# The first gate chunk of a fused attention step, multiplied in two halves of 256 tokens, with its weights loaded ahead of two token tiles

## The chip, the cores and the metric

The kernel runs on one core of a Trainium2 chip. The metric is device time in microseconds, from launch to end. The kernel before takes 711.55 us, the median of three runs (711.53 to 712.34).

## The reference

One step of a hybrid diffusion backbone with one trunk layer. There are 1152 tokens of width 1024: 128 context tokens (tile 0) and 1024 latent tokens (tiles 1 to 8, 128 tokens each). Everything is float32.

```python
shift, scale, gate = modulation(cond, w_mod[l], b_mod[l])      # silu(cond) @ w_mod + b_mod
h = rmsnorm(x, norm_gain[l]) * (1.0 + scale) + shift
q_a, k_a, v_a, g_a, q_b, k_b, v_b, g_b = project(h, w_in[l], ...)
o_a = global_attn_latent(q_a, k_a, v_a, ...)
o_b = window_attn_latent(q_b, k_b, v_b, ..., sink_b[l])
x = x + gate * concat([o_a * silu(g_a), o_b * silu(g_b)]) @ w_out[l]
```

The change touches only the beginning: rmsnorm and modulation of the first token tiles, and the product that gives `g_a`, the gates of head group A (512 columns of `w_in`).

## The kernel before, in words

**Arithmetic.** A matrix product is made of three products of rounded parts: high part of the activations by high part of the weights, high by low, low by high. A high part is a cast (`whi`, `h_at(0, ...)`), the low part is what the cast left out (`wlo`, `h_at(1, ...)`).

**A token tile's way in.** `load_x(t)` (L366) fetches a tile of 128 tokens by 1024 from the SP queue into one of four `xn` buffers. `squares(t)` (L370) has ACT square and sum it (L373) and POOL turn the sum into 1/rms (L375, L377). `scaled(t)` (L379) has DVE multiply the tile by it (L380). `turned_tile(t)` (L382) has PE transpose it in eight 128x128 blocks, four to each of two PSUM banks `px` (L390). `keep(t, c, copy)` (L392) copies bank c into `xT`; ACT takes the first bank and DVE the second, mostly.

**Modulation of a row chunk.** Width 1024 is cut into eight chunks of 128 rows, called k or j. For chunk j, `modulate_rows(j)` (L342) multiplies the condition by the slice `wm[j]` (1 MB, loaded by `load_wm`, in two halves for chunk 0) in 16 small matmuls (L346) and has it copied to `mrows` (L349). `modulate(j)` (L351) transposes that (L355), and DVE makes of it a scale `a_mod` and a shift `b_col` (L357, L359, L361). `modulated(j, t0, n, cond)` (L396) applies them to n tiles from tile t0: ACT writes the high part of h (L403), DVE the same in full (`hf`, L404), POOL the difference (L405).

**Gate products.** `W_GA.load()` (L214) fetches 256 KB of weights for a chunk, `W_GA.split()` (L230) casts them on ACT (L234) and subtracts on DVE or POOL (L236). `gate_products` (L253) makes the three products for one group of 128 gate columns `ch`: high parts at L263 and L264, the low part of h at L259. There are four groups, each with a PSUM bank for tiles 1 to 4 (512 tokens, `big`, through `first_gates`) and a half bank for tiles 5 and 6 (256 tokens, `small`, through `next_gates`); each sums over the eight chunks.

**Order.** Everything is written out by hand; the engines run their instructions in the order of the program, each waiting on semaphores. Ahead of the loop over j (L467), tiles 1 to 4 go through squares, scaling and transposes, chunk 0 is modulated for all four tiles, and its weights are split. Iteration j of the loop makes the gate products of chunk j - 1 for the 512 tokens, has chunk j modulated between them, brings in another tile (tile 5 in j = 1, tile 6 in j = 2, then 7, 8 and 0), and makes the products for tiles 5 and 6 of chunk j - 2. `warm(n)` (L420) issues n matmuls on an identity matrix whose result nobody reads.

**SP queue.** All loads stand in one queue: x tiles 1 to 4, `wm[0]` in two halves, the first gate weights, x tile 5, `wm[1]` and so on (L407 to L418). A load into a buffer waits there until its last reader is through, and every load waits for the one eight places ahead of it to land.

Of the kernel before, what the change touches and what calls it, by code (L numbers as in the profile page):

```python
# [58 lines left out]
WARM = (8, 4)  # L59
# [49 lines left out]
def hybrid_step(ctx, tc, x_prompt, x_sample, cache_k_a, cache_v_a, cache_k_b, cache_v_b,  # L109
# [33 lines left out]
    def bank(tag, name):  # L143
        return ps.tile([P, 512], F32, tag=tag, name=name, bufs=BANKS[tag])
# [108 lines left out]
    def gate_products(out, w, ch, ts, k, first=True, last=True, part=None):  # L253
        cs = slice(P * ch, P * ch + P)
        if part != 1:
            gate_high(out, w, cs, ts, k, first)
        if part != 0:
            i, to = third(ts)
            nc.tensor.matmul(out, w.hi[k][:, cs], h_at(1, i, k, to), start=False, stop=(k == KT - 1 and last))  # L259
# [52 lines left out]
    with tc.tile_pool(name="st", bufs=2, side="right") as st:  # L312
# [11 lines left out]
        def load_wm(j):  # L324
            w = st.tile([P, KT, 2, P], F32, tag="wm", name=f"wm{j}", bufs=3)
            for ks in (slice(0, 4), slice(4, 8)) if j == 0 else (slice(0, 8),):
                nc.sync.dma_start(w[:, ks], w_mod_ss[j][:, ks])
            wm.append(w)
# [13 lines left out]
        def modulate_rows(j):  # L342
            pm = pmod[j] = bank_tr(f"pm{j}")
            for k in range(KT):
                a = 32 * (k % 4)
                nc.tensor.matmul(pm[a : a + 32, 0:256], sil32[:, k, :], wm[j][:, k].rearrange("p s n -> p (s n)"),  # L346
                                 start=(k < 4), stop=(k >= 4), tile_position=(0, a))
            mrows[j] = st.tile([P, 256], F32, tag="mrows", name=f"mrows{j}")
            (nc.scalar.copy if j > 1 else nc.vector.tensor_copy)(mrows[j], pm[:, 0:256])  # L349

        def modulate(j):  # L351
            pm = pmod.pop(j)[:, 256:512]
            for s in range(2):
                cs = slice(P * s, P * s + P)
                nc.tensor.transpose(pm[:, cs], mrows[j][:, cs], ident)  # L355
            m4 = st.tile([P, 2, 2], F32, tag="m4", name=f"m4_{j}")
            nc.vector.tensor_reduce(m4, pm.rearrange("p (s g c) -> p s c g", s=2, c=32)[:, :, 0:2, :], axis=AX.X,  # L357
                                    op=ALU.add)
            nc.vector.tensor_scalar(a_mod[:, j, :], m4[:, 0], bsc1[:, j : j + 1], colt[:, 16 + j : 17 + j],  # L359
                                    op0=ALU.add, op1=ALU.mult)  # L360
            nc.vector.tensor_scalar(b_col[:, j, :], m4[:, 1], colt[:, 24 + j : 25 + j], None, op0=ALU.add)  # L361
# [4 lines left out]
        def load_x(t):  # L366
            xn[t] = st.tile([P, D], F32, tag="xn", name=f"xn{t}", bufs=4)
            nc.sync.dma_start(xn[t], x_tile[t])
# [10 lines left out]
        def scaled(t):  # L379
            nc.vector.tensor_scalar(xn[t], xn[t], rx.pop(t), None, op0=ALU.mult)  # L380

        def turned_tile(t, tags, between=None):  # L382

            for c in range(2):
                if c and between:
                    between()
                px[t, c] = bank(tags[c], f"px{t}_{c}")
                for i in range(4):
                    k = 4 * c + i
                    nc.tensor.transpose(px[t, c][:, P * i : P * i + P], xn[t][:, P * k : P * k + P], ident)  # L390

        def keep(t, c, copy):  # L392
            at = slice(P * place(t), P * place(t) + P)
            copy(xT[:, 4 * c : 4 * c + 4, at], px.pop((t, c)).rearrange("p (k n) -> p k n", n=P))

        def modulated(j, t0, n, cond):  # L396

            w = P * n
            dst = slice(P * place(t0), P * place(t0) + w)
            i, to = third(dst)  # L400
            a, b = (x[:, j, cond : cond + 1] for x in (a_mod, b_col))
            hf = st.tile([P, 512], F32, tag="hf", name=f"hf{j}_{t0}", bufs=3)
            nc.scalar.activation(h_at(0, i, j, to), xT[:, j, dst], AF.Identity, scale=a, bias=b)  # L403
            nc.vector.tensor_scalar(hf[:, :w], xT[:, j, dst], a, b, op0=ALU.mult, op1=ALU.add)  # L404
            nc.gpsimd.tensor_tensor(h_at(1, i, j, to), hf[:, :w], h_at(0, i, j, to), op=ALU.subtract)  # L405

        for t in (1, 2, 3, 4):  # L407
            load_x(t)
        load_wm(0)
        W_GA.load()  # L410
        load_x(5)
        load_wm(1)
        load_x(6)
        W_GA.load()
        load_wm(2)
        W_GA.load()
        load_x(7)
# [2 lines left out]
        def warm(n):  # L420

            idle = bank("D", "idle")
            for _ in range(n):
                nc.tensor.matmul(idle, ident_b, ident_b.unsqueeze(1).to_broadcast([P, 4, P]), start=True, stop=True)

        second = [x for k in range(KT) for x in ((k, 7, 2, 0), (k, 0, 1, 1))]

        def first_gates(ch, k, part=None):
            gate_products(big[ch], W_GA, ch, slice(0, 512), k, part=part)

        def next_gates(ch, k):
            o = 256 * (ch % 2)
# [5 lines left out]

        copies = nc.scalar.copy, nc.vector.tensor_copy

        for t in (1, 2, 3, 4):
            squares(t)
        warm(WARM[0])
        for t, tags in ((1, "AB"), (2, "AB"), (3, "CC")):
            scaled(t)
            turned_tile(t, tags)
            if t > 1:
                for c in range(2):
                    keep(t - 1, c, copies[c])
        scaled(4)  # L450
        modulate_rows(0)
        keep(3, 0, copies[0])
        W_GA.split(nc.gpsimd)
        turned_tile(4, "AB", lambda: modulate(0))
        keep(4, 0, copies[0])
        modulated(0, 1, 4, 0)
        keep(3, 1, copies[1])
        keep(4, 1, copies[1])
        load_wm(3)
        load_x(0)  # L460
        squares(5)
        warm(WARM[1])
        big = [bank("AABB"[ch], f"pg0_{ch}_f") for ch in range(4)]
        sg_tile.append(lambda n: st.tile([P, 512], F32, tag="sg", name=n))
        rest = {3: 7, 4: 8, 5: 0}

        for j in range(1, KT + 2):  # L467
            big_on, small_on = j <= KT, 2 <= j
            if 1 < j < KT:
                W_GA.split()  # L470
            if j == KT + 1:
                put_gates(big[0], 0, 0, slice(0, 512))
            if big_on:
                first_gates(0, j - 1, 0)
                first_gates(1, j - 1, 0)
            if j == 2:
                turned_tile(6, "CC")
                for c in range(2):
                    keep(6, c, copies[c])
                small = [bank("C", f"pg0_{ch}_s") for ch in (0, 2)]  # L480
                for k in range(2):
                    modulated(k, 5, 2, 0)
            if j < KT:
                modulate_rows(j)
                if j + 3 < KT:
                    load_wm(j + 3)
            if j == 1:
                scaled(5)
                squares(6)
            if j in rest:  # L490
                scaled(rest[j])
            if j + 1 in rest:
                squares(rest[j + 1])
            if big_on:
                first_gates(0, j - 1, 1)
                first_gates(1, j - 1, 1)
                first_gates(2, j - 1)
            if j < KT:
                modulate(j)
                if j == 1:  # L500
                    W_GA.split()
                modulated(j, 1, 4, 0)
                if j == 1:
                    scaled(6)
            if big_on:
                first_gates(3, j - 1)
            if j == 1:
                turned_tile(5, "DE")
                for c in range(2):
                    keep(5, c, copies[c])  # L510
            if j in rest:
                turned_tile(rest[j], "DE")
                for c in range(2):
                    keep(rest[j], c, copies[c])
            if 1 < j < KT:
                modulated(j, 5, 2, 0)
            for ch in range(4):
                if small_on:
                    next_gates(ch, j - 2)
                if j > SECOND_FROM or (j == SECOND_FROM and ch % 2):  # L520
                    more()
            if KT - 2 <= j < KT:
                raw = st.tile([P, KT, 2, P], F32, tag="wm", name=f"raw_qa{j}", bufs=3).rearrange(
                    "p (k a) s n -> p k (a s n)", a=2)
                k0 = 4 * (j - KT + 2)
                c0, n = W_QA.cols[0]
                nc.sync.dma_start(
                    raw, w_in[P * k0 : P * k0 + 512, c0 : c0 + n].rearrange("(k p) n -> p k n", p=P))
                W_QA.raw += [raw[:, k] for k in range(4)]
# [816 lines left out]
```

## Time and profile before

| what | value |
|---|---|
| median of three runs | 711.55 us |
| profiled execution, first to last instruction | 709.6 us |
| PE busy | 691.6 us, 97% |
| DVE, ACT, POOL busy | 469.3, 409.9, 334.2 us |
| first transpose of tile 1 | at 8.18 us |
| first gate product | at 16.98 us |
| first gate product of chunk 1 (iteration j = 2) | at 22.34 us |
| `wm[0]` issued from 3.52 us, its second half landed | 8.7 us after its issue |

In the profile PE is the matrix engine, PEld its weight loads, DVE the vector engine, ACT the scalar engine, POOL the GpSimd engine, SP the engine that issues most loads. A row of the timeline has the start in us, the duration in us, the engine, the source line, the operation, the tile written and those read, their shapes, how many instructions are merged (x16: the duration runs from the first's start to the last's end), and in brackets how long the engine sat idle before and who released it. Buffer numbers are left out of names. A matmul's duration overlaps the next one's, so its cost in a row of matmuls is the distance between two starts.

### The profile page before, as it was taken

Reading aid. Unit: us, or ns where it says so; the run is one execution under the profiler, and the core shown is the slowest. Engines: PE = TensorE matmul, PEld = TensorE weight load, DVE = VectorE, ACT = ScalarE, POOL = GpSimd, SP = SyncE. Lnnn points to the kernel's source line nnn. Section 1 sums busy time; section 2 is a strip of 40 time slices with the busy share of each in tenths; the row PEclk is TensorE's granted clock in tenths of the full one; section 3 lists DMA queues with packets and bytes.
Section 4 is the critical chain, followed back from the end, with each engine's and each line's share of the span. In section 5 each row is a group of like instructions: output and inputs, shape, how many; then the busy total and the mean of one; then the engine's idle time right before and its main releaser. Section 6 shows DMA issues by size and latency. Waiting matters only on the chain. (4 is left out here: it accounts for less than half of the span.)

```text
span 709.6 us, 10604 instructions
## 1 busy us (share of the span) xinstructions
PE 691.6 (97%) x3508; PEld 558.5 (79%) x3508; DVE 469.3 (66%) x1019; ACT 409.9 (58%) x829; POOL 334.2 (47%) x356
## 2 busy tenths in 40 slices
PE   7999999999999999989999999999999999999987
PEld 4778988878787889966788888888888888787865
DVE  4667257967848945647867578666775776675662
ACT  5646412412403431188777887787778777877760
POOL 3547023233213421256756655665576557555660
PEclk9999999999999999999999999999999999999999
DMA  8962283358353116332222121212221221222323
GB/s 316 415 211 102 78 302 74 90 154 263 84 139 104 37 39 215 123 108 57 78 68 85 50 82 53 71 57 75 68 82 38 79 71 50 78 72 70 104 67 121
DMA packets 53560, 78.58 MB, mean 111 GB/s; under 512 B 7096, under 2 KB 25720, under 8 KB 52608
## 3 DMA queue, kind: packets, MB, share of 16 engines
q1 hardware_dynamic: 45328, 65.96, 28.1%
q10 hardware_dynamic: 8176, 11.94, 6.3%
q8 instruction: 28, 0.46, 0.3%
q14 instruction: 28, 0.23, 0.1%
HBM read 58.69 MB, written 19.18 MB: 110 GB/s over the span
## 5 line engine op out<-in xcount | busy, mean ns | idle before, releaser
L1131 POOL TENSOR_TENSOR pl<-pe,ph 128x512 fp32r<-128x512 f32 x130 | 167.7, 1292 | 145.0 <-DVE nm L942 67.5
L882 DVE TENSOR_REDUCE mx<-pmx 128x1 f32<-128x384 f32 x192 | 101.4, 552 | 56.3 <-PE pmx L881 54.8
L1123 ACT ACTIVATE pe<-st 128x512 f32<-128x512 f32 x146 | 86.8, 594 | 28.2 <-PE st L1121 27.4
L1127 ACT CAST ph<-pe 128x512 fp32r<-128x512 f32 x146 | 90.6, 621 | 4.8
L1141 PE MATMUL pv<-ph,v_hi 128*128 128x512 f32 x208 | 82.8, 398 | 2.2 <-DVE spare L1165 2.2
L1144 PE MATMUL pv<-pl,v_hi 128*128 128x512 f32 x208 | 82.4, 396 | 0.0
L1212 PE MATMUL po<-wo,ogh 128*128 128x512 f32 x216 | 72.6, 395 | 0.2 <-DVE yt L1219 0.2
L174 POOL TENSOR_TENSOR rs_q<-ms_q,mhalf 128x8 f32<-128x8 f32 x18 | 34.1, 1896 | 80.9 <-DVE ms_q L172 80.9
L942 DVE CUSTOM_DVE_ANT_0 sn<-sn,mask,nsink 128x512 f32<-128x512 f32 (+1 forms) x64 | 46.4, 724 | 38.0 <-PE sn L939 37.6
L881 PE MATMUL pmx<-kha,qt 128*128 128x384 f32 x192 | 61.2, 363 | 0.4 <-ACT pen L928 0.2
L1120 PE MATMUL st<-qt,kha 128*128 128x512 f32 x144 | 58.2, 404 | 1.9 <-ACT pe L1123 1.1
L1121 PE MATMUL st<-qb,kla 68*128 68x512 f32 x144 | 57.5, 399 | 1.1 <-DVE qb L901 1.1
L1143 PE MATMUL pv<-ph,v_lo 128*64 128x512 f32 x146 | 57.6, 395 | 0.0
L1144 PEld LDWEIGHTS pv<-pl,v_hi 128*128 128x128 f32 x208 | 39.2, 189 | 16.4
L928 ACT ACTIVATE pen<-sn,nm 128x512 f32<-128x512 f32 (+2 forms) x72 | 45.0, 626 | 6.5 <-DVE nm L942 3.1
L1116 ACT CAST ph<-st 128x512 fp32r<-128x512 f32 x62 | 36.4, 587 | 19.9 <-PE st L1115 18.7
L1141 PEld LDWEIGHTS pv<-ph,v_hi 128*128 128x128 f32 x208 | 39.3, 189 | 10.6 <-ACT ogh L1177 2.4
L646 ACT CAST qo0q<-ptq 128x512 fp32r<-128x512 f32 x18 | 10.6, 586 | 60.7 <-PE ptq L643 55.8
L1212 PEld LDWEIGHTS po<-wo,ogh 128*128 128x128 f32 x216 | 40.0, 188 | 6.8 <-DVE yt L1219 0.6
L1117 DVE TENSOR_TENSOR pl<-st,ph 128x512 fp32r<-128x512 f32 x62 | 42.5, 686 | 2.7 <-ACT ph L1116 2.1
L1212 PE MATMUL po<-wo,ogl 128*128 128x512 f32 x108 | 42.6, 394 | 0.0
L881 PEld LDWEIGHTS pmx<-kha,qt 128*128 128x128 f32 x192 | 35.6, 191 | 6.4 <-DVE mx L882 1.3
(213 smaller groups left out, 1699.2 us busy)
## 6 DMA issues: line engine op xcount, KB each, us to landing
qt<-qd SPq DMA_DIRECT2D x36, 256.0 KB, 3.0
wm<-in_w_mod_ss_dram SPq DMA_DIRECT2D x7, 1024.0 KB, 10.0
qd<-qo0q ACTq DMA_DIRECT2D x36, 128.0 KB, 2.4
qd<-qo1q ACTq DMA_DIRECT2D x36, 128.0 KB, 2.4
sgl<-gd SPq DMA_DIRECT2D x36, 128.0 KB, 2.2
out_dram<-yt SPq DMA_DIRECT2D x17, 256.0 KB, 2.0
xn<-in_x_sample_dram SPq DMA_DIRECT2D x8, 512.0 KB, 7.2
wg<-in_w_mod_g_dram SPq DMA_DIRECT2D x4, 1024.0 KB, 8.3
```

The costliest lines, as they stand in the source:

```text
L881: nc.tensor.matmul(pm[:, 0:384], lhs, kha[:, g, 3 * b : 3 * b + 3, :], start=True, stop=True)
L882: nc.vector.tensor_reduce(mx[:, h, b : b + 1], pm[:, 0:384], axis=AX.X, op=ALU.max)
L942: nc.vector.tensor_tensor_reduce(s, s, mask[:, m0 : m0 + n], -1.0, nsink[:, 4 * g + h : 4 * g + h + 1], op0=ALU.add, op1=ALU.min, accum_ou ...
L1120: nc.tensor.matmul(s, kh, qtile[i], start=True, stop=False)
L1121: nc.tensor.matmul(s, kl, qbtile[i], start=False, stop=True)
L1123: nc.scalar.activation(pe, s, AF.Exp)
L1127: nc.scalar.copy(ph, pe)
L1131: nc.gpsimd.tensor_tensor(pl, pe, ph, op=ALU.subtract)
L1141: nc.tensor.matmul(pv, two, ph, start=(b == 0), stop=False)
L1143: nc.tensor.matmul(pv[0:64, :], vl, ph, start=False, stop=False)
L1144: nc.tensor.matmul(pv, two, pl, start=False, stop=last)
L1212: nc.tensor.matmul(po[n], a, wo_parts[KT * n + k][lo], start=(k == KS[0] and p == 0), stop=(k == KS[-1] and p == 2))
```

## The change

Loads: x tiles 3 and 4 move behind `wm[0]` and the first gate weights; x tile 5 moves behind `wm[1]` and the second gate weights.

Preparation: only tiles 1 and 2 are squared, scaled and transposed ahead of chunk 0's modulation, and each tile is copied to `xT` right behind its transposes. Chunk 0 is then modulated for tiles 1 and 2 alone, and the products of its high parts with the first 256 tokens are issued. Tiles 3 and 4 are squared behind that modulation, transposed around the products of the low part, and modulated as a second half. The other 256 tokens of chunk 0 are multiplied in the loop's first iteration, where all 512 were before. Chunks 1 to 7 are multiplied by 512 tokens as before. The number of gate products of chunk 0 goes from 12 with 512 tokens to 24 with 256.

```diff
-        for t in (1, 2, 3, 4):
+        for t in (1, 2):
             load_x(t)
         load_wm(0)
         W_GA.load()
+        for t in (3, 4):
+            load_x(t)
+        load_wm(1)
+        W_GA.load()
         load_x(5)
-        load_wm(1)
         load_x(6)
-        W_GA.load()
         load_wm(2)
         W_GA.load()
         load_x(7)
@@
-        def first_gates(ch, k, part=None):
-            gate_products(big[ch], W_GA, ch, slice(0, 512), k, part=part)
+        def first_gates(ch, k, part=None, half=None):
+            ts = slice(0, 512)
+            if k == 0:
+                ts = slice(256 * (half or 0), 512 if half is None else 256 * half + 256)
+            gate_products(big[ch][:, ts], W_GA, ch, ts, k, half != 1, part=part)
@@
-        for t in (1, 2, 3, 4):
+        for t in (1, 2):
             squares(t)
         warm(WARM[0])
-        for t, tags in ((1, "AB"), (2, "AB"), (3, "CC")):
+        for t, tags in ((1, "AB"), (2, "CC")):
             scaled(t)
             turned_tile(t, tags)
-            if t > 1:
-                for c in range(2):
-                    keep(t - 1, c, copies[c])
+            for c in range(2):
+                keep(t, c, copies[c])
+        big = [bank("AABB"[ch], f"pg0_{ch}_f") for ch in range(4)]
+        modulate_rows(0)
+        W_GA.split(nc.gpsimd)
+        modulate(0)
+        modulated(0, 1, 2, 0)
+        squares(3)
+        squares(4)
+        warm(WARM[1])
+        for ch in range(4):
+            first_gates(ch, 0, 0, 0)
+        scaled(3)
+        turned_tile(3, "CC")
+        for c in range(2):
+            keep(3, c, copies[c])
+        for ch in range(4):
+            first_gates(ch, 0, 1, 0)
         scaled(4)
-        modulate_rows(0)
-        keep(3, 0, copies[0])
-        W_GA.split(nc.gpsimd)
-        turned_tile(4, "AB", lambda: modulate(0))
-        keep(4, 0, copies[0])
-        modulated(0, 1, 4, 0)
-        keep(3, 1, copies[1])
-        keep(4, 1, copies[1])
+        turned_tile(4, "DE")
+        for c in range(2):
+            keep(4, c, copies[c])
+        modulated(0, 3, 2, 0)
         load_wm(3)
         load_x(0)
         squares(5)
-        warm(WARM[1])
-        big = [bank("AABB"[ch], f"pg0_{ch}_f") for ch in range(4)]
@@
-                first_gates(0, j - 1, 0)
-                first_gates(1, j - 1, 0)
+                first_gates(0, j - 1, 0, 1)
+                first_gates(1, j - 1, 0, 1)
```

The remaining calls of `first_gates` in the loop get the same last argument, 1.

The order of ACT ahead of the loop is the first place that matters. In the kernel before, `xn_177`, `xn_179`, `xn_181` and `xn_183` are x tiles 1 to 4, `px_0_*` is the first transposed half of a tile, `whiga` the cast weights, `h_0_0` the high part of h for chunk 0:

```order
L373 ACTIVATE sq_206,ss_207<-xn_177 128x1024
L373 ACTIVATE sq_213,ss_214<-xn_179 128x1024
L373 ACTIVATE sq_220,ss_221<-xn_181 128x1024
L373 ACTIVATE sq_227,ss_228<-xn_183 128x1024
L394 COPY xT<-px_0_244 128x4x128
L394 COPY xT<-px_0_255 128x4x128
L394 COPY xT<-px_0_268 128x4x128
L234 CAST whiga_293<-rawga_188 128x512
L394 COPY xT<-px_0_299 128x4x128
L403 ACTIVATE h_0_0_115<-xT,b_col,a_mod 128x512
L373 ACTIVATE sq_326,ss_327<-xn_190 128x1024
```

In the changed kernel x tiles 3 and 4 are `xn_186` and `xn_188`:

```order
L373 ACTIVATE sq_206,ss_207<-xn_177 128x1024
L373 ACTIVATE sq_213,ss_214<-xn_179 128x1024
L394 COPY xT<-px_0_230 128x4x128
L394 COPY xT<-px_0_243 128x4x128
L234 CAST whiga_270<-rawga_184 128x512
L403 ACTIVATE h_0_0_115<-xT,b_col,a_mod 128x256
L373 ACTIVATE sq_286,ss_287<-xn_186 128x1024
L373 ACTIVATE sq_293,ss_294<-xn_188 128x1024
L394 COPY xT<-px_0_314 128x4x128
L394 COPY xT<-px_0_331 128x4x128
L403 ACTIVATE h_0_0_115<-xT,b_col,a_mod 128x256
```

The squares of tiles 3 and 4 have moved from ahead of the first copy to behind the first modulated h, and h comes in two pieces.

DVE in the same place is the second. Before, with `xn` as above, `rsx` the 1/rms of a tile, and `px_1_*` the second transposed half of a tile:

```order
L380 TENSOR_SCALAR xn_177<-xn_177,rsx_211 128x1024
L380 TENSOR_SCALAR xn_179<-xn_179,rsx_218 128x1024
L394 COPY xT<-px_1_249 128x4x128
L380 TENSOR_SCALAR xn_181<-xn_181,rsx_225 128x1024
L394 COPY xT<-px_1_260 128x4x128
L380 TENSOR_SCALAR xn_183<-xn_183,rsx_232 128x1024
L349 COPY mrows_290<-pm_281 128x256
L357 TENSOR_REDUCE m_0_306<-pm_281 128x4
L359 TENSOR_SCALAR a_mod<-m_0_306,bsc_170,colt 128x2
L361 TENSOR_SCALAR b_col<-m_0_306,colt 128x2
L404 TENSOR_SCALAR hf_1_316<-xT,a_mod,b_col 128x512
```

And in the changed kernel:

```order
L380 TENSOR_SCALAR xn_177<-xn_177,rsx_211 128x1024
L394 COPY xT<-px_1_235 128x4x128
L380 TENSOR_SCALAR xn_179<-xn_179,rsx_218 128x1024
L394 COPY xT<-px_1_248 128x4x128
L349 COPY mrows_268<-pm_259 128x256
L357 TENSOR_REDUCE m_0_278<-pm_259 128x4
L359 TENSOR_SCALAR a_mod<-m_0_278,bsc_170,colt 128x2
L361 TENSOR_SCALAR b_col<-m_0_278,colt 128x2
L404 TENSOR_SCALAR hf_1_282<-xT,a_mod,b_col 128x256
L380 TENSOR_SCALAR xn_186<-xn_186,rsx_291 128x1024
L394 COPY xT<-px_1_319 128x4x128
L380 TENSOR_SCALAR xn_188<-xn_188,rsx_298 128x1024
```

The copy of tile 1's second half now stands between the scalings of tiles 1 and 2, and the scalings of tiles 3 and 4 stand behind the first modulation, with the copy of tile 3 between them.

More of the change, by code (lines that the diff above doesn't have):

```diff
@@ L494, in hybrid_step @@
             if big_on:
-                first_gates(0, j - 1, 1)
-                first_gates(1, j - 1, 1)
-                first_gates(2, j - 1)
+                first_gates(0, j - 1, 1, 1)
+                first_gates(1, j - 1, 1, 1)
+                first_gates(2, j - 1, None, 1)
             if j < KT:
@@ L505, in hybrid_step @@
             if big_on:
-                first_gates(3, j - 1)
+                first_gates(3, j - 1, None, 1)
             if j == 1:
```

## The prediction

> **What bounds the kernel now.** I read first how busy each engine is in the stages around the change, then the timelines of PE, ACT, DVE and POOL ahead of the loop, then the loads. The stages:
>
> ```profile
> 0.00:16.98 16.98, 11.89 (x63) 7.25 (x63) 7.17 (x17) 9.82 (x17) 5.27 (x15) 1.00 0.85 312
> 16.98:22.34 5.36, 5.36 (x38) 3.62 (x39) 3.47 (x9) 3.52 (x7) 2.79 (x5) 1.00 1.03 420
> 22.34:61.00 38.66, 38.59 (x288) 29.35 (x288) 29.41 (x55) 23.19 (x46) 22.41 (x27) 1.00 0.68 256
> 61.00:200.00 139.00, 138.89 (x689) 115.27 (x690) 95.42 (x184) 41.51 (x77) 39.58 (x31) 1.00 0.47 143
> 200.00:400.00 200.00, 194.44 (x977) 160.64 (x976) 132.32 (x326) 104.11 (x224) 88.00 (x88) 1.00 0.31 94
> 400.00:709.60 309.60, 302.42 (x1457) 242.37 (x1455) 201.46 (x432) 227.73 (x464) 176.16 (x194) 1.00 0.23 73
> ```
>
> After stretch and length the columns are busy PE, PEld, DVE, ACT, POOL, granted clock, DMA share, GB/s. From 16.98 us, where the first gate product starts, PE does not pause until 61 us. So the start is a question of one instant: when does PE enter iteration j = 2 (22.34 us before), with the same work left? From there on the programs are alike. PE before that:
>
> ```profile
> 3.36 3.60 PE L424 MATMUL idle<-ident_b 128*128 128x512 bf16 x8 [3.36 <-DVE ident_b L316]
> 8.18 3.68 PE L390 MATMUL px<-ident,xn 128*128 128x128 f32 x16 [1.22 <-DVE xn L380]
> 13.29 1.07 PE L346 MATMUL pm<-wm,sil 128*32 128x256 f32 x16
> 14.91 0.44 PE L355 MATMUL pm<-ident,mrows 128*128 128x128 f32 x2
> 15.19 0.60 PE L390 MATMUL px<-ident,xn 128*128 128x128 f32 x4
> 16.98 0.50 PE L263 MATMUL pg_f<-h,whiga 128*128 128x512 f32 x1 [0.33 <-ACT h L403]
> 17.32 0.40 PE L264 MATMUL pg_f<-h,wloga 128*128 128x512 f32 x1
> 17.56 0.40 PE L263 MATMUL pg_f<-h,whiga 128*128 128x512 f32 x1
> 18.12 1.07 PE L346 MATMUL pm<-wm,sil 128*32 128x256 f32 x16
> 21.30 1.03 PE L390 MATMUL px<-ident,xn 128*128 128x128 f32 x8
> 22.34 0.50 PE L263 MATMUL pg_f<-h,whiga 128*128 128x512 f32 x1
> ```
>
> Two things: the first gate product waits for ACT's h, and tiles 1 and 2 went through PE back to back, 16 transposes in 3.68 us, when eight take 1.03 us later. PE starts at half speed, though the granted clock reads 1.00 throughout.
>
> [...]
>
> **The chain that the change makes.** What a tile needs, taken from tile 3 (first five rows) and from copies and chunk 0's modulation:
>
> ```profile
> 9.13 1.06 ACT L373 ACTIVATE sq<-xn 128x1024 bf16<-128x1024 f32 x1 [1.36 <-DMA xn<-in_x_sample_dram]
> 10.09 0.19 ACT L373 ACTIVATION_READ_ACCUMULATOR sq<-xn 128x1 f32 x1
> 10.37 0.19 POOL L375 TENSOR_SCALAR msx<-ss 128x1 f32<-128x1 f32 x1 [1.54 <-ACT sq L373]
> 10.64 0.55 POOL L377 TENSOR_TENSOR rsx<-msx,mhalf 128x1 f32<-128x1 f32 x1
> 11.22 0.76 DVE L380 TENSOR_SCALAR xn<-xn,rsx 128x1024 f32<-128x1024 f32 x1 [0.34 <-POOL rsx L377]
> ...
> 8.86 0.76 DVE L380 TENSOR_SCALAR xn<-xn,rsx 128x1024 f32<-128x1024 f32 x1 [0.73 <-POOL rsx L377]
> 10.19 0.69 DVE L394 COPY xT<-px 128x512 f32<-128x512 f32 x1 [0.58 <-PE px L390]
> 12.96 0.59 ACT L394 COPY xT<-px 128x512 f32<-128x512 f32 x1 [0.32 <-PE px L390]
> 16.11 0.81 ACT L403 ACTIVATE h<-xT,b_col,a_mod 128x512 fp32r<-128x512 f32 x1 [0.54 <-DVE b_col L361]
> 24.63 1.09 ACT L403 ACTIVATE h<-xT,b_col,a_mod 128x256 fp32r<-128x256 f32 x2
> ```
>
> *Tile 2.* DVE now copies tile 1 ahead of scaling tile 2. The copy cannot start before 10.19, when tile 1's transposes end; it ends at 10.88, the scaling at 11.64 (9.62 before). PE, which went straight on, idles, and transposes tile 2 from 11.65 at the slow rate (8.18 to 10.15 was eight): 13.6.
>
> *Modulation.* Its 16 small matmuls follow. At full speed they take 1.07 us; no row shows them slow, so the bounds are 0.8 us (1.07, overlapping the transposes' end by a quarter microsecond) and 1.8 (1.97 / 1.03 = 1.9 times, same overlap). I take 1.8, PE having just paused: 15.4. From their end (13.29 + 1.07 = 14.36) to h was 1.75 us before; the slow pair at L355 adds some 0.2: h starts at 17.35 and, half as wide, takes 1.09 / 2 = 0.55: 17.9. The first gate products therefore start no earlier than the 16.98 of before.
>
> *Tile 3.* ACT squares tile 3 only behind that h, where before it did so at 9.13. Squares to read-out are 1.15 us (9.13 to 10.28), POOL 0.91 (to 11.19), DVE 0.79 (to 11.98): 17.9 + 2.85 = 20.75. PE meanwhile has its four idle matmuls and eight half-width products, and then waits. POOL's low part of h lies in front of tile 3's mean but ends within the squares:
>
> ```profile
> 25.91 1.48 POOL L405 TENSOR_TENSOR h<-hf,h 128x256 fp32r<-128x256 f32 x2 [1.61 <-DVE hf L404]
> ```
>
> Two of that width take 1.48 us, so one takes 0.74, against 1.15 for the squares.
>
> *Tile 4.* Tile 3's transposes, 1.03 at full speed: 21.8. DVE copies (0.7), then scales tile 4 (0.76): 23.3. The first four transposes (0.60) end at 23.9, ACT copies (0.59) and makes the second half of h (0.55): with hand-offs 25.1. DVE's copy of tile 4 and the four low-part products lie beside this.
>
> *Iteration j = 1.* Products of 256 tokens cost half (the first two rows; the others are ACT's, in j = 1 of before):
>
> ```profile
> 27.64 0.28 PE L264 MATMUL pg_s<-h,wloga 128*128 128x256 f32 x1
> 27.75 0.28 PE L259 MATMUL pg_s<-h,whiga 128*128 128x256 f32 x1
> 20.10 0.60 ACT L234 CAST whiga<-rawga 128x512 fp32r<-128x512 f32 x1
> 21.47 0.82 ACT L403 ACTIVATE h<-xT,b_col,a_mod 128x512 fp32r<-128x512 f32 x1 [0.77 <-DVE b_col L361]
> ```
>
> Start to start 0.11 to 0.12, against 0.24 (17.32 to 17.56) for 512 tokens: twice as many at half the price, nothing on PE's total. Four products bring the second modulation to 25.6, its matmuls to 26.65. Before, 3.15 us lay between their end (19.19) and 22.34, with five wide products ahead of the transposes of its rows; those now save 0.6: 26.65 + 2.55 = 29.2. ACT has tile 5's and 6's squares and a weight cast in between, 2 x 1.15 + 0.6 behind 25.1 = 28.0, before h is due to start, at 28.3 (as much ahead of 29.2 as 21.47 of 22.34). **Sum: 29.2 - 22.34 = 6.9 us late.**
>
> **Loads**, which the change also moves:
>
> ```profile
> L327 SPq DMA_DIRECT2D wm<-in_w_mod_ss_dram x2: 471/537/603, 3.5 to 4.2; - x2
> DMA to landing us min/median/max: 8.7/8.7/8.7
> DMA to landing us min/median/max: 6.4/6.8/7.2
> ...
> 13.89 2.25 SPq L368 DMA_DIRECT2D xn<-in_x_sample_dram x2
> 17.66 0.33 SPq L327 DMA_DIRECT2D wm<-in_w_mod_ss_dram x1
> 29.97 0.42 PE L346 MATMUL pm<-wm,sil 128*32 128x256 f32 x4
> wm<-in_w_mod_ss_dram SPq DMA_DIRECT2D x7, 1024.0 KB, 10.0
> ```
>
> The first pair of rows is `wm[0]`: its second half landed at 4.2 + 8.7 = 12.9. The next row is x tiles 3 and 4 (issued 2.6 and 3.05, landed by 10.3). Without these 1 MB in front, at 312 to 420 GB/s, `wm[0]` lands 2.5 to 3.4 us earlier, about 10. That gains nothing, since tile 2's transposes end at 13.6. Tiles 3 and 4 land 3 to 4 us later, by some 14, which ACT's other work up to 17.9 hides; were that cover gone, each microsecond would cost one. Loads of tiles 7 and 8 (13.89 on, 2.25) wait for buffers of tiles 3 and 4, now until 21.8 and 24; the fourth `wm` (17.66) is queued behind them, to about 25. With the usual 10.0 to land it is there at 35; its matmuls (29.97) are wanted 6.9 later, at 36.9. Cover 1.9 us.
>
> **Forecast.** The profiled execution has 709.6 us of span, the median is 711.55, so 1.95 lie outside. Span 709.6 + 6.9 = 716.5; time 711.55 + 6.9 = **718.4 us**.
>
> **Rivals.**
>
> *PE stays slow longer.* If the pauses (half a microsecond at 15.5, the wait for tile 3) keep PE slow until it runs without pause from about 24, tile 3 costs 0.9 more, half of tile 4 0.5, four products 0.45, the second modulation 0.95: 2.8 more, **721.2**. For it: the eight idle matmuls, 3.60 us without pause, did not suffice. Against: PE works some 8 us from 11.65 to 20.1 with one short gap. In the kernel before, PE was slow until tile 2 was through at 11.86 and then fast for the 16 small matmuls at 13.29, so some 4 to 5 us of work from 8.18 on sufficed there. Chance 0.21. [...]
>
> *PE is fast from tile 2 on.* Tile 2 saves 0.9, the small matmuls 1.0, their transposes 0.2: 2.1 less, **716.3**. Against: the pause at 10.15 to 11.65. Chance 0.12.
>
> *Faster.* Twelve half-width products (1.4 us) are done before PE's unbroken stretch. If the second half of h were ready when PE wants it, about 16.98, PE would start that stretch with 1.4 us less to do: 711.55 - 1.4 = **710.1**. It decides at tile 4's transposes, which would have to end by 15.8 as they did before (15.19 + 0.60). For it: both tiles have landed by 14. Against: ACT runs its squares behind h. Chance 0.04.
>
> *The delay is made up later.* PE idles 0.11 + 5.56 + 7.18 = 12.85 us behind 61 us. If the 5.56 between 200 and 400 us were waits on something that does not move with PE, 6.9 would shrink to 1.3: 712.9, or to nothing. Loads take 0.31 of the DMA time there, so it is not they; engines fed by PE move with it. Chance 0.05, 0.03 of it within 0.2%.
>
> That leaves 0.58 for the forecast. The range goes from 715.9, under the early-fast case by 0.4 for some ten hand-offs, to 721.3. A measurement here can tell 0.2% (1.4 us) from no change: faster 0.04, same 0.03, slower 0.93.
>
> **What the new profile would show.** Right: the first 256-token product near 18 and no earlier than 16.98, ACT's third square behind the first h, PE released by DVE's scaling ahead of tile 3 near 20.7, the second half of h near 25, j = 2 entered near 29, and no PE wait on a load. If tile 3's eight transposes take about 2 us, the slow rival holds. Wrong: tile 3's square before h, or j = 2 entered before 24.

## The result, and the profile after

The changed kernel takes 720.48 us, the median of four runs (719.09 to 721.33), against 711.54 (711.39 to 712.34): ratio 1.0108, 95% interval 1.0086 to 1.0131. It is 8.9 us slower, inside the range and in the direction forecast, 2.1 us beyond the point forecast. The profiled execution took 721.33 with a span of 719.5.

The stages of the changed kernel, cut where its own stages end (same columns as before: length, busy PE, PEld, DVE, ACT, POOL, granted clock, DMA share, GB/s):

```profile
0.00:16.98 16.98, 10.33 (x46) 4.92 (x46) 5.21 (x14) 6.01 (x11) 3.59 (x11) 0.80 0.86 320
16.98:25.00 8.02, 5.72 (x29) 4.96 (x28) 2.10 (x3) 3.43 (x7) 2.47 (x5) 0.69 0.73 282
25.00:31.00 6.00, 5.55 (x33) 3.73 (x33) 2.51 (x7) 3.30 (x6) 2.23 (x5) 0.55 0.73 232
```

Two things have changed. From 16.98 to 25 us PE is busy for 5.72 of 8.02, where it did not pause before. And the granted clock, 1.00 in every stage before, is 0.55 to 0.80 until 31 us. From there PE is at full speed again (granted clock 1.00), but for one stretch of 3.4 us at 317 us (0.50), and the two programs run alike.

PE's timeline to the entry into iteration j = 2 (22.34 before, 32.08 now):

```profile
3.33 3.43 PE L426 MATMUL idle<-ident_b 128*128 128x512 bf16 x8 [3.33 <-DVE ident_b L316]
8.09 1.09 PE L390 MATMUL px<-ident,xn 128*128 128x128 f32 x8 [1.33 <-DVE xn L380]
10.62 1.97 PE L390 MATMUL px<-ident,xn 128*128 128x128 f32 x8 [1.45 <-DVE xn L380]
12.52 1.94 PE L346 MATMUL pm<-wm,sil 128*32 128x256 f32 x16
17.11 0.38 PE L263 MATMUL pg_f<-h,whiga 128*128 128x256 f32 x1
19.94 1.79 PE L390 MATMUL px<-ident,xn 128*128 128x128 f32 x8 [1.62 <-DVE xn L380]
23.27 1.94 PE L390 MATMUL px<-ident,xn 128*128 128x128 f32 x8 [0.68 <-DVE xn L380]
26.82 1.94 PE L346 MATMUL pm<-wm,sil 128*32 128x256 f32 x16
32.08 0.50 PE L263 MATMUL pg_f<-h,whiga 128*128 128x512 f32 x1 [0.20 <-ACT h L403]
```

The first gate product comes at 17.11, no earlier than the 16.98 of before. Ahead of tiles 2, 3 and 4 PE waits for DVE's scaling. And the same eight transposes take 1.09 or 1.8 to 1.97, the same 16 small matmuls 1.94 both times (1.07 before). The entry is 9.7 us late, the span 9.9 us longer.

ACT and DVE around the three waits, in the timeline of all engines:

```profile
9.22 0.69 DVE L394 COPY xT<-px 128x512 f32<-128x512 f32 x1 [1.19 <-PE px L390]
9.82 0.74 DVE L380 TENSOR_SCALAR xn<-xn,rsx 128x1024 f32<-128x1024 f32 x1
...
16.45 0.60 ACT L403 ACTIVATE h<-xT,b_col,a_mod 128x256 fp32r<-128x256 f32 x1 [3.58 <-DVE b_col L361]
16.96 1.04 ACT L373 ACTIVATE sq<-xn 128x1024 bf16<-128x1024 f32 x1
19.04 0.75 DVE L380 TENSOR_SCALAR xn<-xn,rsx 128x1024 f32<-128x1024 f32 x1 [2.16 <-POOL rsx L377]
21.77 0.69 DVE L394 COPY xT<-px 128x512 f32<-128x512 f32 x1 [1.98 <-PE px L390]
22.38 0.74 DVE L380 TENSOR_SCALAR xn<-xn,rsx 128x1024 f32<-128x1024 f32 x1
25.01 0.60 ACT L403 ACTIVATE h<-xT,b_col,a_mod 128x256 fp32r<-128x256 f32 x1
```

These are the forecast's hand-overs: tile 2 scaled behind tile 1's copy, tile 3 squared behind the first h, tile 4 scaled behind tile 3's copy, the second half of h at the end of it.

### The profile page after: what moved, and what is told of

It is laid out like the page before. It is cut to its first block, busy times and chain, and to the rows that moved or that the text cites. A ratio compares the mean times of both kernels' runs of the same rounds, so it can differ in the third digit from the quotient of the medians.

```text
span 719.5 us, 10632 instructions
## 1 busy us (share of the span) xinstructions
PE 697.8 (97%) x3520; PEld 562.6 (78%) x3520; DVE 469.3 (65%) x1020; ACT 410.4 (57%) x830; POOL 334.9 (47%) x357
```

## The experiments

Main theory: a chain of waits that the new order of ACT and DVE makes, lengthened where its pauses let PE fall to half speed. Rivals: the new order of loads, or the 256-token products. Times stand beside the kernel before on the same chip: 712.04 for the repeat, the loads, the halves and the squares; 711.67 for the order of work, tile 1's copies, the filled pauses and the three moves; 711.82 for the last two.

**The changed kernel again.** No edit.

> The changed kernel once more, nothing altered. If the chain of waits alone set its time (squares of tile 3 behind the first h, copy of tile 1 ahead of scaling tile 2), the times should repeat within 0.5 us and PE enter iteration j = 2 at 32.1 us again. If PE's slow first microseconds have a part in it (its pauses let it fall back to half speed, at a moment that differs from run to run), the times spread over 1 to 2 us, 719 to 721.5, and this profile shows other groups of transposes slow (eight in about 2 us) than the first one did, with the entry into j = 2 moved by as much.

720.11 us (719.06 to 721.13), ratio 1.0107 (1.0081 to 1.0132). Its profiled run, 719.85 us:

```profile
10.60 1.84 PE L390 MATMUL px<-ident,xn 128*128 128x128 f32 x8 [1.45 <-DVE xn L380]
19.54 1.06 PE L390 MATMUL px<-ident,xn 128*128 128x128 f32 x8 [1.62 <-DVE xn L380]
22.14 1.06 PE L390 MATMUL px<-ident,xn 128*128 128x128 f32 x8 [1.06 <-DVE xn L380]
24.93 1.94 PE L346 MATMUL pm<-wm,sil 128*32 128x256 f32 x16
29.91 0.50 PE L263 MATMUL pg_f<-h,whiga 128*128 128x512 f32 x1 [0.21 <-ACT h L403]
```

Tiles 3 and 4 are fast here, where the first profile had them slow, and j = 2 is entered 2.2 us earlier. The difference of the two entries is PE's speed, not the chain. (The span is only 1.4 us shorter: the other 0.8 went into one wait near 230 us, where PE waits 2.1 us for DVE ahead of the keys' transposes, 1.3 in the first profile. Why DVE is later there stays open.)

**Loads only, in the kernel before.**

```diff
-        for t in (1, 2, 3, 4):
+        for t in (1, 2):
             load_x(t)
         load_wm(0)
         W_GA.load()
+        for t in (3, 4):
+            load_x(t)
+        load_wm(1)
+        W_GA.load()
         load_x(5)
...
```

> The kernel before with nothing but the changed order of loads. If the delay comes from the order of ACT and DVE (chain theory), later tiles 3 and 4 cost here what their squares, which still stand ahead of ACT's copies, wait longer: tile 3 lands near 12.1 instead of 9.0, so the first gate product moves from 17.0 to about 19.7, 2.8 us or, with PE slow, up to 4.5: 714.3 to 716. If the later arrival of tiles 3 and 4 is the whole loss (load theory), it shows all 8.9: 720.5.

716.9 us (715.93 to 718.62), ratio 1.0058 (1.0034 to 1.0082), a little over the upper end expected.

```profile
12.12 1.06 ACT L373 ACTIVATE sq<-xn 128x1024 bf16<-128x1024 f32 x1 [4.42 <-DMA xn<-in_x_sample_dram]
15.03 1.97 PE L390 MATMUL px<-ident,xn 128*128 128x128 f32 x8 [3.72 <-DVE xn L380]
21.93 0.50 PE L263 MATMUL pg_f<-h,whiga 128*128 128x512 f32 x1 [0.33 <-ACT h L403]
```

In the old order of work, ACT waits 4.42 us for tile 3 and PE, at half speed since 9.90 (granted clock 0.50 until 20.14), idles 3.72 us. The first gate product is 4.95 us late. So the loads alone do harm, but not all of it.

**The order of work only, with the loads of before.** The same edit reversed, in the changed kernel.

> The changed kernel's order of work with the loads in the order of before (x tiles 1 to 4 first). Chain theory: the squares of tile 3 wait for the first h, not for their data, so tiles 3 and 4 landing 3 us earlier help nothing, and the first weights landing near 13 instead of 10 hold the first modulation up by at most 1 us: 720 to 721.5, as slow as the whole change or slower. Load theory: the loss goes away, 711.5 to 713.

720.23 us (718.47 to 721.47), ratio 1.011 (1.0077 to 1.0143): as slow as the whole change. ACT:

```profile
17.09 0.60 ACT L403 ACTIVATE h<-xT,b_col,a_mod 128x256 fp32r<-128x256 f32 x1 [3.28 <-DVE b_col L361]
17.59 1.04 ACT L373 ACTIVATE sq<-xn 128x1024 bf16<-128x1024 f32 x1
```

ACT sits idle for 3.28 us and then does h and the square in that order, though tile 3 is loaded early again. With this order the loads neither cost nor gain anything that the runs can tell (720.1 to 720.5 with the new ones), and the load theory falls: the order of work alone makes the whole delay.

**Halves only, in the kernel before.** Chunk 0 is multiplied in two halves, both in j = 1:

```diff
-            gate_products(big[ch], W_GA, ch, slice(0, 512), k, part=part)
+            for half in range(2) if k == 0 else (None,):
+                ts = slice(0, 512) if half is None else slice(256 * half, 256 * half + 256)
+                gate_products(big[ch][:, ts], W_GA, ch, ts, k, half != 1, part=part)
```

> The kernel before, with chunk 0 multiplied in two halves of 256 tokens in the place where it was multiplied whole; loads and all else as before. Chain theory: 24 products at half the price, no change, 711.5 within 0.7. If narrow products cost more than half (a weight load for each that no longer hides), up to 12 x 0.12 = 1.4 us more: 713.

712.24 us, ratio 1.0005 (0.9991 to 1.0019). No change. The interval of 1 us either way would hide a part of the 1.4 us of the rival, but the profile does not: it enters j = 2 at 22.25, against 22.34. Narrow products cost half, as reckoned (0.12 us from start to start at full speed, as at 17.96 and 18.08 with only the order of work changed, against 0.24 for 512 tokens).

**Squares of tiles 3 and 4 ahead of the first h.**

```diff
         W_GA.split(nc.gpsimd)
+        squares(3)
+        squares(4)
         modulate(0)
         modulated(0, 1, 2, 0)
-        squares(3)
-        squares(4)
```

> The changed kernel with the squares of tiles 3 and 4 ahead of the first h on ACT (behind the weight cast), all else as in it. Chain theory: tile 3 is scaled right behind the first h's other half, its transposes start near 18.2 instead of 19.9, 1.8 us earlier, up to 3 if PE stays fast because its longest pause is gone: 717.5 to 718.7. Load theory: tiles 3 and 4 arrive as late as before, no change: 720.5.

717.42 us (716.16 to 718.12), ratio 1.0061 (1.0036 to 1.0086): 2.7 us back, where the chain alone was to give 1.8 and PE's speed the rest of up to 3.

```profile
18.69 1.03 PE L390 MATMUL px<-ident,xn 128*128 128x128 f32 x8
21.27 1.06 PE L390 MATMUL px<-ident,xn 128*128 128x128 f32 x8 [1.06 <-DVE xn L380]
27.53 0.50 PE L263 MATMUL pg_f<-h,whiga 128*128 128x512 f32 x1 [0.21 <-ACT h L403]
```

Tile 3's transposes follow the gate products without a wait. Tile 4 still waits for its scaling behind tile 3's copy.

**Tile 1's copies behind tile 2's transposes**, as they were before:

```diff
             turned_tile(t, tags)
+        for t in (1, 2):
             for c in range(2):
                 keep(t, c, copies[c])
```

> The changed kernel with the copies of tile 1 behind the transposes of tile 2, as they were before, all else as in it. Chain theory: tile 2 is scaled by 9.6 instead of 10.6 and PE loses its first pause, so 1.0 us earlier: 719.1. If PE's half speed has its part: up to 2 us more where tile 2 and the small matmuls run fast, 717 to 719. If DVE's copy was beside the path: no change, 720.1.

718.73 us (718.02 to 719.2), ratio 1.009 (1.0063 to 1.0117).

```profile
7.99 3.68 PE L390 MATMUL px<-ident,xn 128*128 128x128 f32 x16 [0.98 <-DVE xn L380]
28.64 0.50 PE L263 MATMUL pg_f<-h,whiga 128*128 128x512 f32 x1 [0.21 <-ACT h L403]
```

That is 1.4 us less than the 720.1 of the change, or 1.0 when each is set against the kernel before on its own chip (7.1 and 8.1 us slower). The intervals overlap, so the times alone do not show the gain. The profile shows the wait gone: tiles 1 and 2 go through PE back to back. How much of the gain is chain and how much PE's speed, these runs cannot tell.

**PE's pauses filled** with 16 more idle matmuls:

```diff
-WARM = (8, 4)
+WARM = (10, 4)
...
             turned_tile(t, tags)
+            warm({1: 5, 2: 0}[t])
...
             first_gates(ch, 0, 0, 0)
+        warm(6)
         scaled(3)
...
             first_gates(ch, 0, 1, 0)
+        warm(3)
         scaled(4)
```

> The changed kernel with 16 more idle matmuls in PE's pauses: 2 more at the start, 5 behind tile 1's transposes, 6 ahead of tile 3's, 3 ahead of tile 4's. If PE's fall to half speed costs 2 to 4 us of the delay, PE stays at full speed from tile 1 or 2 on and enters j = 2 near 27 to 28: 715.5 to 717.5. If the chain of ACT, POOL and DVE alone sets the time, the idle matmuls gain nothing or delay it where they outlast the pause: 720 to 722.

716.41 us (715.76 to 717.7), ratio 1.0063 (1.0044 to 1.0082).

```profile
10.54 1.09 PE L390 MATMUL px<-ident,xn 128*128 128x128 f32 x8 [0.36 <-DVE xn L380]
17.77 1.09 PE L390 MATMUL px<-ident,xn 128*128 128x128 f32 x8 [0.21 <-DVE xn L380]
20.40 1.06 PE L390 MATMUL px<-ident,xn 128*128 128x128 f32 x8 [0.40 <-DVE xn L380]
23.01 1.07 PE L346 MATMUL pm<-wm,sil 128*32 128x256 f32 x16
26.67 0.50 PE L263 MATMUL pg_f<-h,whiga 128*128 128x512 f32 x1 [0.21 <-ACT h L403]
```

Work that nobody reads makes the kernel 3.7 to 4.1 us faster. Every group is at its fast duration (the granted clock is 1.00 throughout), and what remains, 716.41 - 711.67 = 4.7 us, is the chain by itself.

**Three moves undone at once**, loads and halves kept. A fourth goes with them: the low-part products move behind tile 4's transposes.

```diff
             turned_tile(t, tags)
+        for t in (1, 2):
             for c in range(2):
                 keep(t, c, copies[c])
...
         W_GA.split(nc.gpsimd)
-        modulate(0)
-        modulated(0, 1, 2, 0)
         squares(3)
         squares(4)
+        modulate(0)
+        scaled(3)
+        modulated(0, 1, 2, 0)
+        scaled(4)
...
-        scaled(3)
         turned_tile(3, "CC")
...
-        for ch in range(4):
-            first_gates(ch, 0, 1, 0)
-        scaled(4)
         turned_tile(4, "DE")
...
+        for ch in range(4):
+            first_gates(ch, 0, 1, 0)
         modulated(0, 3, 2, 0)
```

> The changed kernel with loads and halves kept and three moves undone at once: copies of tile 1 behind tile 2's transposes, squares of tiles 3 and 4 ahead of the first h, and both scalings ahead of tile 3's copy, so that no tile waits for another's copy. Chain theory: tile 3 is transposed by 18.5, tile 4 right behind, the second half of h is there near 20, and j = 2 is entered at 23.5 to 25: 712.5 to 714.5. Halves or loads to blame: no better than 717.

713.68 us (712.6 to 715.39), ratio 1.0024 (1.001 to 1.0038).

```profile
15.65 0.39 PE L263 MATMUL pg_f<-h,whiga 128*128 128x256 f32 x1 [2.19 <-ACT h L403]
16.71 2.02 PE L390 MATMUL px<-ident,xn 128*128 128x128 f32 x16
23.93 0.50 PE L263 MATMUL pg_f<-h,whiga 128*128 128x512 f32 x1 [0.21 <-ACT h L403]
```

Tiles 3 and 4 go through PE back to back, and most of the loss is gone. The first gate product is 1.3 us earlier than in the kernel before, and j = 2 is still entered 1.6 us later. (The profiled run is the slowest of the ten; another 2.4 us went behind 225 us, where its granted clock is 0.50 from 232.36 to 235.77.)

**The first h between the two squares**, in that kernel:

```diff
         squares(3)
-        squares(4)
         modulate(0)
         scaled(3)
         modulated(0, 1, 2, 0)
+        squares(4)
```

> The reordered kernel with ACT's first h between the squares of tiles 3 and 4 instead of behind both. There the scale and shift were ready at 13.4 and h waited until 15.0 for the squares, the first of which waited for tile 3 to land. If that wait is what is left of the delay, the first gate product comes at 14.4 instead of 15.65 and j = 2 is entered up to 0.5 us earlier, 713.2. If what is left sits behind tile 4 (its square, scaling, transposes, copy and second h, one after another), j = 2 is entered at 23.9 as before, or later where tile 4's square is later: 713.7 to 714.3.

714.39 us (713.79 to 715.85), ratio 1.0033 (1.0022 to 1.0043).

```profile
18.73 1.06 PE L390 MATMUL px<-ident,xn 128*128 128x128 f32 x8 [1.49 <-DVE xn L380]
25.00 0.50 PE L263 MATMUL pg_f<-h,whiga 128*128 128x512 f32 x1 [0.21 <-ACT h L403]
```

The first gate product comes at 15.15, half a microsecond earlier still (although tiles 1 and 2 ran slowly in this run), and j = 2 later by 1.1: PE now waits 1.49 us for tile 4's scaling. About half of the 1.1 is the slow tiles' doing (an estimate: h starts at 14.50, and could have started when tile 3's square was read out, at 13.98). The medians, 714.39 and 713.68, do not differ by more than the noise. What is left sits behind tile 4. An earlier start of the gates is worth nothing while the last tile is late. No version here points below the kernel before.

**Three more idle matmuls in the kernel before**, over the 1.2 us pause at its start:

```diff
-WARM = (8, 4)
+WARM = (11, 4)
```

> The kernel before with three more idle matmuls at its start, 11 instead of 8, which bridge the 1.2 us pause ahead of tile 1's transposes, so that PE can be at full speed from tile 1 on. If half speed is on the path only where the change put it there (before, tile 3 waits for its scaling and chunk 0's small matmuls for a load that lands at 12.9), faster transposes of tiles 1 and 2 gain nothing: first gate product at 17.0 within 0.3, 711.7 within 0.7. If PE's slow start also costs the kernel before something, tiles 1 and 2 save 2 x 0.9: 710.

711.97 us, ratio 1.0001 (0.9987 to 1.0014).

```profile
8.16 1.09 PE L390 MATMUL px<-ident,xn 128*128 128x128 f32 x8
16.62 0.50 PE L263 MATMUL pg_f<-h,whiga 128*128 128x512 f32 x1 [0.32 <-ACT h L403]
21.97 0.50 PE L263 MATMUL pg_f<-h,whiga 128*128 128x512 f32 x1
```

Eight transposes take 1.09 us from tile 1 on, the first gate product comes at 16.62 instead of 16.98, j = 2 is entered at 21.97 instead of 22.34, and the time is the same within 1 us. Of the 1.8 us that tiles 1 and 2 might have saved, 0.4 reached j = 2. Half speed cost little (0.4 us) where it stood beside the path, and the change put it on the path.

## Why the prediction held, and where it was short

**The chain** was right. Forecast and profile, in us: first gate product near 18 and not before 16.98, measured 17.11 (16.70 in the second profile, a little under the bound); ACT's square of tile 3 behind h at 16.96; square to transposes 2.85 against 19.94 - 16.96 = 2.98; second half of h complete at 25.1 against 25.01 + 0.60 = 25.6. That tile 2 would wait for tile 1's copy, tile 3 for the first h and tile 4 for tile 3's copy was tested by undoing them: 1.4 us for the first, 2.7 for the second, all three together (with the low-part products moved) 720.1 to 713.7. The third was not undone alone, and the 1.4 is not clear of noise.

Two errors cancel in the 25.6, and that is luck. The forecast counted tile 1 as slow, as it was in the kernel before (1.97 us for eight transposes), but in both profiles of the changed kernel it took 1.09, which brings all that follows 0.9 us forward; in the first profile the slow tiles 3 and 4 then lose more than that. The case that the forecast describes did occur, with the loads of before: in the profile with only the order of work changed, tiles 1 and 2 and the small matmuls are slow and PE is fast (granted clock 1.00) from 15.65 to 237 us. There the first gate product comes at 17.74 (forecast 17.9), tile 3's transposes start at 20.57 (20.75), the second half's first product at 25.10 (25.1), and j = 2 is entered at 29.43 (29.2).

**PE's speed** is the term that was too small. The forecast charged half speed for tile 2 and the small matmuls, 2.1 us, and took PE to be fast from tile 3 on. The small matmuls' 1.8 us were the author's estimate, on the ground that PE had just paused; that a pause alone makes them slow no run shows. They took 1.94 in the first profile and 1.93 in the second. The runs give 3.7 to 4.1 for all of it (720.1 to 720.5 against 716.41 with the pauses filled), so 1.6 to 2.0 were missing, nearly all of the 2.1 between 718.4 and 720.5. The rival with PE fast from tile 2 on was priced at 716.3, and the filled kernel took 716.41 (with tile 1 fast as well, which that price did not have); the rival with PE slow until after tile 4 was priced at 721.2, and the execution with tiles 3 and 4 slow took 721.33. Which of them a run gets is settled anew each time. The step that failed was the argument that some 8 us of work make PE fast and that it then stays so. Here is the start of the changed kernel's first profile, cut where the granted clock changes and, where it stays for longer, every 3.41 us:

```profile
6.45:9.87 3.42, 1.40 (x10) 0.86 (x8) 1.41 (x3) 1.74 (x3) 1.59 (x4) 1.00 0.99 325
9.87:13.28 3.41, 2.66 (x16) 1.97 (x20) 1.35 (x3) 1.10 (x2) 0.32 (x1) 0.50 1.06 436
13.28:16.69 3.41, 2.86 (x17) 1.07 (x10) 1.28 (x6) 0.23 (x1) 0.95 (x1) 0.50 1.00 401
16.69:20.11 3.42, 1.80 (x12) 1.21 (x11) 0.94 (x2) 2.55 (x5) 2.10 (x5) 1.00 1.04 426
20.11:23.52 3.41, 2.73 (x14) 2.46 (x13) 1.35 (x2) 0.59 (x1) 0.37 (x1) 0.50 0.52 179
23.52:26.94 3.42, 2.97 (x16) 2.34 (x19) 1.01 (x2) 2.44 (x5) 0.54 (x1) 0.50 0.44 144
26.94:30.35 3.41, 3.41 (x24) 2.14 (x25) 1.09 (x2) 1.45 (x3) 1.69 (x5) 0.50 0.92 287
```

The clock is 1.00 or 0.50 for a whole stretch and changes only at its end: at 9.87, 16.69, 20.11 and 30.35 us, which lie 6.82, 3.42 and 10.24 apart, one, two or three times some 3.41. PE did become fast at 16.69, after 2.86 us of work in 3.41, as argued. But in the next stretch it waits 1.62 us for tile 3, works 1.80 of 3.42, and falls back for the next 10 us. The stretches ahead of the two falls were 41% and 53% busy.

**The granted clock** reads 1.00 over the slow transposes of the kernel before, and the forecast noted this without a reason. In the changed kernel the column does show half speed, from 9.87 on. But the eight idle matmuls at 3.33, 3.43 us long, run as slowly as the 3.60 of before (where four of them take 1.03 at 15.62) under a 1.00 (0 to 6.45 us): a 1.00 at the very start tells nothing. The trace's first record of the clock stands at 6.45 us here and at 12.56 in the kernel before, behind its slow transposes.

**Loads.** No wait of PE on a load, as forecast. That the weights' earlier landing gains nothing and the later landing of tiles 3 and 4 costs nothing here is borne out by putting the loads back (720.23). In the old order of work the same loads cost 4.9 us, because there ACT squares tile 3 ahead of everything.

**Faster, or made up later:** neither. The entry into j = 2 was 9.7 us late and the span 9.9 us longer, so nothing came back. Nor did it in the profiles of the kernels made from the changed one: each ended with the delay that it had at j = 2 and up to 3.0 us more.

## What to carry to other kernels

Before moving work ahead, follow what is thereby moved behind it on each in-order engine: here one early h on ACT pushed two squares back and two copies on DVE pushed two scalings back, and through POOL, DVE and PE that became 4.7 us of chain. What counts at the start is when the last input is ready and PE need not wait again, not when the first product is issued. Where PE will wait now, reckon with half speed for several microseconds behind the wait as well (10 in the first profile); idle matmuls in the pauses show cheaply how much of a loss that is (here 3.7 to 4.1 us).

## What the runs showed of the hardware

In these profiles PE fell to half speed (granted clock 0.50) after stretches of 3.41 us in which it was busy for only a part of the time, and not only at the start. In the second profile of the changed kernel:

```profile
17.61:21.02 3.41, 1.79 (x15) 1.46 (x13) 1.14 (x2) 1.82 (x4) 1.72 (x4) 1.00 1.00 407
21.02:24.44 3.42, 1.49 (x12) 1.23 (x12) 1.98 (x4) 1.61 (x3) 0.05 (x1) 1.00 0.71 202
24.44:27.85 3.41, 3.41 (x25) 1.92 (x23) 0.91 (x2) 2.27 (x5) 2.17 (x5) 0.50 0.96 360
```

After 1.79 busy of 3.41 PE stayed at full speed, after 1.49 of 3.42 it did not; in the first profile it did not after 1.80 either. Over the twelve profiles, their last 10 us left out, PE fell 13 times, each time after a stretch with 1.28 to 2.15 us busy, and it kept its full speed through others with as little as 1.54 (19.06 to 22.48 us with only the order changed) and 1.67 (13.90 to 17.32 with the three moves undone). So the busy time of a stretch does not tell a fall by itself; what does stays open. In the first profile PE rose after 2.86 and 3.41 busy, and not after 2.66, 2.73 and 2.97. Where the stretches begin differs from run to run (the first recorded fall stands at 9.87 us in the first profile, at 10.78 in the second), and with it which work runs slowly: the two profiles of the one program enter j = 2 at 32.08 and 29.91.

The same happens far behind the change. In the kernel with only the order of work changed, around a pause of PE of 2.06 us (it waits for DVE ahead of the keys' transposes; 1.25 us in the profile of before):

```profile
234.10:237.50 3.40, 1.34 (x9) 0.90 (x8) 3.37 (x14) 0.15 (x1) 1.69 (x2) 1.00 0.49 177
237.50:240.90 3.40, 3.40 (x10) 2.62 (x9) 3.33 (x12) 1.05 (x4) 1.00 (x1) 0.50 0.02 5
```

That profiled execution took 721.47 us although it had entered j = 2 at 29.43, earlier than the two of the change. Runs of the kernel before on the same chips reached from 710.94 to 714.94. Such falls can make this spread: the profile with halves only, nearly the same program, entered j = 2 at 22.25, ran at a granted clock of 0.50 from 308.34 to 315.17, and had a span 2.0 us longer than the kernel before (713.36 us). None of the slower runs of the kernel before itself was profiled.
